# The first layer's scale vector by dot products on VectorE, its shift still by matrix products on TensorE

## The chip, the core and the metric

The kernel runs on one NeuronCore of a Trainium2 chip. The metric is the device time of one execution in microseconds (us), lower is better. The engines are named as the profile names them: PE is TensorE (PEld its weight loads), DVE is VectorE, ACT is ScalarE, POOL is GpSimd, and SP is the engine whose queue issues nearly all DMAs.

## What is computed

Two layers of a trunk over 128 context and 512 latent tokens of width 1024. Every layer is modulated by vectors that are made from two conditioning vectors (one for context, one for latent tokens) and a weight matrix `w_mod`. The change touches only how the first two of these vectors are made for the first layer.

```python
mod_ctx = (silu(c_ctx) @ w_mod[l] + b_mod[l])        # 6 * 1024 values
mod_lat = (silu(c)     @ w_mod[l] + b_mod[l])
sh1, sc1, gt1, sh2, sc2, gt2 = split(mod, 6)
h = rmsnorm(x, g_pre_mix) * (1 + sc1) + sh1
... = split_in(h @ w_in)                              # all branches of the layer start here
```

`sh1` is called the shift and `sc1` the scale below. Nothing of layer 0 can start on PE before `h` exists, and `h` needs both.

## The kernel before

Activations are kept transposed: 8 tiles `x[k]` of 128 channels by 640 tokens. A weight block is 128 output columns by 1024 inputs (512 KB). It is loaded into a ring of three buffers called `raw`, and `wblock` splits it into a high part `wh` (a cast on ACT) and a low part `wl` (a subtraction on DVE or POOL). `h[k]` is split likewise by `split`, a cast on ACT and a subtraction on DVE, and each product is three matmuls: high by high, high by low, low by high.

The order of work is not written by hand. A recorder collects all operations, and `schedule` places them by a list scheduler with modelled costs and due times. Nearly every instruction is issued through line 529, so rows are told apart by tile names, not by lines. Every engine then runs its own list in order.

The prologue (lines 923 to 975) is what the change touches:

- The 8 tiles of x are loaded, squared on ACT and summed, and `stat` makes the rms factor `rsb` of every token with small matmuls on PE and a power on POOL.
- `conv_blocks(0)` loads and splits the first four weight blocks of `win`. They are used by `first_k`, which adds one tile `h[k]` into seven accumulators: for 256 tokens four products (`pp` tiles, 12 matmuls of 256 columns), for the other 384 tokens three (`ps` tiles, 9 matmuls of 384 columns). `proj_half` makes the eighth accumulator, 24 more matmuls of 384 columns.
- For every k, the loop of line 951 makes the scale (j = 1) and then the shift (j = 0) of 128 channels. `half_tiles` loads the 512 KB block of `wmod0` as two tiles `u` of 256 KB, and 8 float32 matmuls of 2 columns each (`ps<-cc,u`; the trace has two records for each, so 16) add into two columns of one PSUM tile `gp`. A DVE instruction adds the bias (`mod<-ps,par`). `der` is (1 + scale) * gain. ACT then makes x * der + shift (two instructions, 512 and 128 tokens), and `split` gives `h[k]`.
- `cond()` loads `crow`, the two conditioning vectors spread over all partitions, into `cb` and applies Silu. It stands behind the loop, since before the change only the later vectors need it.

Those later vectors are made by `modvec`: one 512 KB block in a `raw` buffer, and two dot products on DVE (`tensor_tensor_reduce`; `CUSTOM_DVE_ANT_0` in the trace, `ISA` in the lists of order), one with each conditioning vector. The first dot writes its unused product to a `junk` tile, the second over the block itself, after which the buffer is free.

The first work behind the prologue is the key projection of head 0: products of 320 columns with the fifth weight block of `win`.

Of the kernel before, what the change touches and what calls it, by code (L numbers as in the profile page):

```python
# [11 lines left out]
F32 = mybir.dt.float32  # L12
F32R = mybir.dt.float32r
AF = mybir.ActivationFunctionType
ALU = mybir.AluOpType
AX = mybir.AxisListType

P = 128
D = 1024
KD = D // P  # L20
# [36 lines left out]
NSUM = 2  # L57
# [475 lines left out]
def trunk_kernel(ctx: ExitStack, tc: tile.TileContext, xT, crow, ccol, wmod, wmod0, win, wv, wa, wc, wattn, wo, wff1, wff2,  # L533
# [4 lines left out]
    nc = Recorder(tc.nc)  # L538

    def pool(name, bufs=1, psum=False):  # L540
        kw = dict(space=bass.MemoryType.PSUM) if psum else {}
        return Pool(ctx.enter_context(tc.tile_pool(name=name, bufs=bufs, **kw)), bufs, psum)
# [3 lines left out]
    wp = pool("wp")  # L546
    up = pool("up")
    sm = pool("sm")
# [6 lines left out]
    def nm(s):  # L555
        uid[0] += 1
        return f"{s}_{uid[0]}"

    def U(dt=F32, w=T):
        return up.tile([P, UW], dt, tag="U", name=nm("u"), bufs=NU)[:, :w]  # L560

    def PP():
        return psP.tile([P, 2, 512], F32, tag="P", name=nm("pp"))

    def PS():
        return psS.tile([P, 512], F32, tag="S", name=nm("ps"))
# [218 lines left out]
    def hl():  # L785
        return U(F32R), U(F32R)
# [102 lines left out]
    cb = cst.tile([P, 2, D], F32, name="cb")  # L889

    def cond():
        for g in range(2):
            nc.sync.dma_start(cb[:, g], crow[:, g, :])
            nc.scalar.activation(cb[:, g], cb[:, g], AF.Silu)

    def modvec(l, st, j):

        p, mod, der = st
        part = sm.tile([P, KD, 2], F32, tag="part", name=nm("part"), bufs=2)
        for m in range(KD):  # L900
            r = raw_load(wmod[l, j * KD + m])
            for g in range(2):
                junk = r if g else wp.tile([P, KD * P], F32, tag="sum", name=nm("junk"), bufs=NSUM)
                nc.vector.tensor_tensor_reduce(out=junk, in0=r, in1=cb[:, g], op0=ALU.mult, op1=ALU.add, scale=1.0,
                                               scalar=0.0, accum_out=part[:, m, g:g + 1])
            yield
        sl = mod[:, j * KD:(j + 1) * KD, :]
        o = OFF["b_mod"][0] + j * KD
        nc.vector.tensor_add(sl, part, p[:, o:o + KD, None].to_broadcast([P, KD, 2]))
        which = {1: (0, "g_pre_mix"), 2: (1, "g_post_mix"), 4: (2, "g_pre_mlp"), 5: (3, "g_post_mlp")}.get(j)  # L910
        if which is not None:
            i, gn = which
            g = pr(p, gn)[:, :, None].to_broadcast([P, KD, 2])
            if j in (1, 4):
                nc.vector.scalar_tensor_tensor(der[:, i], sl, 1.0, g, op0=ALU.add, op1=ALU.mult)
            else:
                nc.vector.tensor_mul(der[:, i], sl, g)
# [7 lines left out]
    p, mod, der = st[0]  # L925
# [5 lines left out]
    cc = sm.tile([P, KD, 2], F32, tag="cc", name=nm("cc"), bufs=1)  # L931
    nc.sync.dma_start(cc, ccol.rearrange("p (a b) -> p a b", b=2))
    nc.scalar.activation(cc, cc, AF.Silu)
    rsb = U()
    for a, b in PART:
        ((rs, _, _),) = stat(sq, a, b, inv[D], True, cuts=((0, b - a),))
# [1 line left out]
    wbs = conv_blocks(0)  # L938
    h = [hl() for _ in range(KD)]
    gp = PS()  # L940
    ts = [PP() for _ in range(2)]
    lead = [[ts[i // 2][:, i % 2, :TP] for i in range(4)], [PS()[:, :T - TP] for _ in range(3)]]
    DH = D // 2

    def half_tiles(src):
        r = [U(w=DH) for _ in range(2)]
        for i in range(2):
            nc.sync.dma_start(r[i], src[:, i * DH:(i + 1) * DH])
        return r

    for k in range(KD):
        nc.either.tensor_mul(x[k], x[k], rsb)
        for j in (1, 0):
            i0 = j * KD + k
            r = half_tiles(wmod0[i0])
            sl = mod[:, i0, :]
            o = OFF["b_mod"][0] + i0
            nc.begin()
            for i in range(KD):
                c = (i % 4) * P  # L960
                nc.tensor.matmul(gp[:, 2 * i0:2 * i0 + 2], r[i // 4][:, c:c + P], cc[:, i, :], start=(i == 0),
                                 stop=(i == KD - 1))
            nc.done()
            nc.vector.tensor_scalar(sl, gp[:, 2 * i0:2 * i0 + 2], p[:, o:o + 1], None, op0=ALU.add)
        o = OFF["g_pre_mix"][0] + k
        nc.vector.tensor_scalar(der[:, 0, k, :], mod[:, KD + k, :], 1.0, p[:, o:o + 1], op0=ALU.add, op1=ALU.mult)
        t = U()
        for s, e, g in ((0, TC, 0), (TC, T, 1)):
            nc.scalar.activation(t[:, s:e], x[k][:, s:e], AF.Identity, bias=mod[:, k, g:g + 1], scale=der[:, 0, k, g:g + 1])
        split(t, *h[k])  # L970
        for hf in range(2):
            first_k(lead[hf], wbs, h, hf, k)
    nc.sync.dma_start(rp, rope)
    cond()
    lead[1].append(proj_half(wbs[3], h, 1, parts=PART))
    xsrc = xT

    for l in range(DEPTH):
        p, mod, der = st[l]
# [33 lines left out]
        for hf in range(2):  # L1013
            for j in range(2):
                pg, pa = lead[hf][2 * j:2 * j + 2]
                a = PART[hf][0]
                for s, e, _ in PSEG[hf]:
                    o = gt[j][:, pos(s):pos(s) + e - s]
# [25 lines left out]
        for i in range(2):  # L1044
            nc.vector.tensor_tensor_reduce(out=U(w=QK), in0=lv[:, 2 * i], in1=lv[:, 2 * i + 1], op0=ALU.mult,
                                           op1=ALU.add, scale=1.0, scalar=0.0, accum_out=ls[:, i:i + 1])
# [215 lines left out]
        for it in range(NH + 1):  # L1262
# [18 lines left out]
            if pend is not None:  # L1281
                hd = it - 1
                pa, pc, ps0 = pend
                o = values(pa, pc, v[0][hd % 2], v[1][hd % 2])
# [95 lines left out]
        o = []  # L1380
        for hd in range(NH):
            r = U()
# [27 lines left out]
        m = []  # L1410
# [170 lines left out]
def _blocks(w):  # L1581

    K, M = w.shape
    return w.reshape(K // P, P, M // P, P).transpose(2, 1, 0, 3).reshape(M // P, P, K)
# [35 lines left out]
def _layout(inp):  # L1620
    a = {k: np.asarray(v) for k, v in inp.items()}
    L = DEPTH
    out = {}
    xall = np.concatenate([a["x_prompt"][0], a["x_sample"][0]], 0)
    out["xT"] = xall.T.reshape(KD, P, T)
    out["crow"] = np.broadcast_to(np.stack([a["c_ctx"], a["c"][0]])[None], (P, 2, D))
    out["ccol"] = np.stack([a["c_ctx"], a["c"][0]], 1).reshape(KD, P, 2).transpose(1, 0, 2).reshape(P, 2 * KD)
    w0 = a["w_mod"][0][:, :2 * D]
    out["wmod0"] = _blocks(w0)
    out["wmod"] = a["w_mod"].transpose(0, 2, 1).reshape(L, 6 * KD, P, D)  # L1630
    win, wv = [], []
    for l in range(L):
        w = a["w_in"][l]
        qp = (np.arange(2 * NH)[:, None] * QK + _DPERM[None]).reshape(-1)
        cols = np.concatenate([np.arange(0, 1536), 1536 + qp, 2560 + qp, np.arange(4608, 8704)])
        win.append(_blocks(w[:, cols]))
        v = w[:, 3584:4608].reshape(2, 4, P, 4, 2 * P)
        wv.append(v.transpose(3, 0, 2, 1, 4).reshape(8, P, D))
    out["win"] = np.stack(win)
    out["wv"] = np.stack(wv)  # L1640
    out["wa"] = np.stack([_pairs(a["sc_w_out"][l]) for l in range(L)])
    out["wc"] = np.stack([_pairs(a["cf_w_out"][l]) for l in range(L)])
    out["wattn"] = np.stack([_blocks(a["attn_w_out"][l]) for l in range(L)])
    out["wo"] = np.stack([_blocks(a["w_o"][l]) for l in range(L)])
    f0, f1 = FD * P, (NF - FE) * P
    out["wff1"] = np.stack([np.concatenate([_blocks(w[:, :f0]), _quads(w[:, f0:], KD)]) for w in a["w_ff1"]])
    ff2 = []
    for w in a["w_ff2"]:
        ff2.append(np.concatenate([_quads(w[:f1], KD), _blocks(w[f1:])]))
    out["wff2"] = np.stack(ff2)  # L1650

    def col(v):
        return v.reshape(-1, P).T

    pars = []
    for l in range(L):
        d = {
            "g_pre_mix": col(a["g_pre_mix"][l]), "g_post_mix": col(a["g_post_mix"][l]),
            "g_pre_mlp": col(a["g_pre_mlp"][l]), "g_post_mlp": col(a["g_post_mlp"][l]), "b_mod": col(a["b_mod"][l]),
            "sc_w": a["sc_conv_w"][l].reshape(SC_K, SCT, P).transpose(2, 1, 0).reshape(P, -1),  # L1660
            "cf_w": a["cf_conv_w"][l].reshape(CF_K, CFT, P).transpose(2, 1, 0).reshape(P, -1),
            "cf_b": col(a["cf_conv_b"][l]), "ln_g": col(a["cf_ln_g"][l]), "ln_b": col(a["cf_ln_b"][l]),
            "cf_b_out": col(a["cf_b_out"][l]), "subln": col(a["subln_g"][l]),
            "lam": np.broadcast_to(np.concatenate([a["lam_q1"][l], a["lam_k1"][l], a["lam_q2"][l], a["lam_k2"][l]])[None],
                                   (P, 4 * QK)),
        }
        pars.append(np.concatenate([d[n] for n, _ in PARAMS], 1))
    out["par"] = np.stack(pars)
    out["ck"] = a["cache_k"][0].transpose(0, 2, 3, 4, 1)[:, :, :, _DPERM].reshape(L, NH, P, P)
    out["cv"] = a["cache_v"][0].reshape(L, P, D)  # L1670
    out["rope"] = _rope_tables()
    return {k: np.ascontiguousarray(v) for k, v in out.items()}
# [28 lines left out]
```

## Time and profile before

| | us |
|---|---|
| median of 3 runs | 2597.32 (2591.19 to 2600.37) |
| the profiled execution | 2599.19 |
| span of its trace | 2597.4 |

PE is busy for 2488.8 us of the span. The profile's page gives busy time for each engine and for 40 equal slices of the span, the TensorE clock that was granted in each, and the chain of waits that ended last. The prologue is the first two slices of 65 us.

### The profile page before, as it was taken

The page shows a single profiled execution, that of the slowest core. Times are in us where ns is not written, and L with a number is a line of the kernel's source. Part 1 is how long each engine was busy: PE and PEld are TensorE (multiplying, and loading weights), DVE is VectorE, ACT ScalarE, POOL GpSimd, SP SyncE. Part 2 cuts the span into 40 slices and gives each one's busy share as a digit, 9 for nine tenths or more (in the row PEclk, how much of TensorE's full clock was granted, in tenths as well). Part 3 has the DMA queues.
Part 4 walks back from the last instruction along what each step waited for, and adds up shares of the span by engine and source line. Part 5 has one row for each costly group of instructions (what it writes and reads, how often), then busy time and mean ns, then how long its engine had stood idle before and what let it go on. Part 6 is the DMA issues. An engine that isn't in the chain of part 4 may idle for free.

```text
span 2597.4 us, 42157 instructions
## 1 busy us (share of the span) xinstructions
PE 2488.8 (96%) x16596; PEld 2412.5 (93%) x16596; DVE 1911.8 (74%) x3104; ACT 1250.4 (48%) x2323; POOL 290.7 (11%) x227
## 2 busy tenths in 40 slices
PE   7999999999999999999999999999999999999998
PEld 7988889999999899998988888999999999999998
DVE  3289786977785698878566887969566748677874
ACT  3365564223223566765445655532232247667653
POOL 1022110001020100012011211000011100001121
PEclk8899999999999999999989999999999999999999
DMA  7122222235554344577523222213454532447671
GB/s 269 48 93 65 66 68 71 87 127 194 176 178 138 99 166 175 191 176 187 171 87 97 76 62 77 73 56 115 154 174 137 175 110 96 140 156 210 176 216 56
DMA packets 132875, 336.76 MB, mean 130 GB/s; under 512 B 16244, under 2 KB 39108, under 8 KB 132676
## 3 DMA queue, kind: packets, MB, share of 16 engines
q1 hardware_dynamic: 122308, 315.19, 36.5%
q0 software_dynamic: 10368, 18.88, 4.3%
q8 instruction: 130, 2.13, 0.3%
q14 instruction: 69, 0.57, 0.1%
HBM read 284.15 MB, written 41.46 MB: 125 GB/s over the span
## 4 chain that ended last, share of the span: by engine, by line
PE 77%; DVE 11%; DMA 5%; ACT 4%; issue 2%; SPq 1%; POOL 0%; DVEq 0%; ACTq 0%; POOLq 0%
PE ps L529 41%; PE pp L529 35%; DVE u L529 8%; ACT u L529 3%; DMA raw<-in_wff_dram 2%; DMA u<-fd 2%; DVE w L529 1%; ACT w L529 1%; DVE mx L529 1%; DMA u<-u 1%; DVE sum L529 1%; SPq L529 1%; DMA u<-on 0%; DMA u<-rqd 0%; POOL st L529 0%
## 5 line engine op out<-in xcount | busy, mean ns | idle before, releaser
L529 PE MATMUL pp<-u,w 128*128 128x320 f32 (+1 forms) x6912 | 1069.6, 312 | 26.3 <-DVE u L529 12.9
L529 PE MATMUL ps<-u,w 128*128 128x320 f32 (+2 forms) x6672 | 1066.2, 315 | 12.1 <-DVE u L529 6.9
L529 PEld LDWEIGHTS pp<-u,w 128*128 128x128 f32 x6912 | 1030.1, 191 | 35.4 <-ACT u L529 13.6
L529 PEld LDWEIGHTS ps<-u,w 128*128 128x128 f32 x6672 | 1010.0, 191 | 25.0 <-DVE u L529 9.2
L529 ACT CAST w<-raw 128x1024 fp32r<-128x1024 f32 (+1 forms) x364 | 313.7, 863 | 290.2 <-PE ps L529 154.6
L529 DVE TENSOR_TENSOR w<-raw,w 128x1024 fp32r<-128x1024 f32 (+1 forms) x271 | 302.6, 1118 | 170.1 <-ACT w L529 166.7
L529 DVE TENSOR_TENSOR u<-u,u 128x640 fp32r<-128x640 f32 (+8 forms) x443 | 324.3, 744 | 72.8 <-ACT u L529 68.4
L529 ACT CAST u<-u 128x640 fp32r<-128x640 f32 (+2 forms) x280 | 195.5, 703 | 156.2 <-DVE u L529 79.7
L529 DVE SCALAR_TENSOR_TENSOR u<-u,par,u 128x640 f32<-128x640 f32 (+13 forms) x272 | 225.8, 863 | 1.7
L529 ACT ACTIVATE u<-u 128x320 f32<-128x320 f32 (+3 forms) x232 | 138.6, 612 | 117.8 <-DVE u L529 109.3
L529 DVE TENSOR_TENSOR w<-sum,w 128x512 fp32r<-128x512 f32 x208 | 143.4, 697 | 43.2 <-ACT w L529 42.2
L529 ACT CAST w<-sum 128x512 fp32r<-128x512 f32 x208 | 127.2, 621 | 87.2 <-PE pp L529 36.5
L529 ACT ACTIVATE u<-pp 128x640 f32<-128x640 f32 (+4 forms) x96 | 52.1, 552 | 234.1 <-PE pp L529 223.3
L529 POOL TENSOR_TENSOR u<-u,u 128x640 f32<-128x640 f32 (+4 forms) x60 | 104.6, 1747 | 503.2 <-DVE u L529 302.1
L529 DVE TENSOR_TENSOR u<-u,ps 128x320 f32<-128x320 f32 (+4 forms) x230 | 106.7, 481 | 52.8 <-PE ps L529 52.2
L529 DVE TENSOR_TENSOR u<-ps,u 128x512 fp32r<-128x512 f32 (+6 forms) x206 | 98.3, 505 | 59.8 <-PE ps L529 33.9
L529 DVE CUSTOM_DVE_ANT_0 junk<-raw,cb 128x1024 f32<-128x1024 f32 x80 | 102.5, 1283 | 46.7 <-DMA raw<-in_wmod_dram 46.5
L529 POOL DMA_DIRECT2D w<-in_wff_dram x72 | 62.9, 873 | 612.9 <-DVE sum L529 361.6
L529 PE MATMUL ps<-w,u 128*128 128x256 f32 x960 | 127.7, 291 | 2.8 <-ACT vo L529 2.8
L529 ACT ACTIVATE u<-pp,mx 128x640 f32<-128x640 f32 x128 | 101.0, 793 | 58.4 <-DVE mx L529 57.4
L529 PEld LDWEIGHTS ps<-w,u 128*128 128x128 f32 x960 | 120.9, 197 | 6.9 <-ACT vo L529 4.0
L529 POOL TENSOR_TENSOR w<-raw,w 128x1024 fp32r<-128x1024 f32 x21 | 52.9, 2521 | 565.6 <-ACT w L529 459.9
(90 smaller groups left out, 1874.5 us busy)
## 6 DMA issues: line engine op xcount, KB each, us to landing
raw<-in_wff_dram SPq DMA_DIRECT2D x128, 512.0 KB, 3.9
raw<-in_win_dram SPq DMA_DIRECT2D x120, 512.0 KB, 3.3
raw<-in_wmod_dram SPq DMA_DIRECT2D x80, 512.0 KB, 3.4
fd<-u SPq DMA_DIRECT2D x64, 320.0 KB, 2.4
u<-fd SPq DMA_DIRECT2D x64, 320.0 KB, 5.6
w<-in_wff_dram POOLq DMA_DIRECT2D x72, 256.0 KB, 5.8
u<-in_wmod_dram SPq DMA_DIRECT2D x32, 256.0 KB, 6.1
raw<-in_wv_dram SPq DMA_DIRECT2D x16, 512.0 KB, 3.3
```

The source lines that it names most:

```text
L529: getattr(eng, m)(*[r(v) for v in a], **{x: r(v) for x, v in k.items()})
```

## The change

The scale blocks of `wmod0` are stored transposed, loaded into the `raw` ring as 512 KB tiles, and multiplied with the two rows of `cb` by two dot products on DVE (a new helper `dots`, taken out of `modvec`). The shift is made as before. `cond()` moves ahead of the loop.

```diff
+    def dots(r, out):
+        for g in range(2):
+            junk = r if g else wp.tile([P, KD * P], F32, tag="sum", name=nm("junk"), bufs=NSUM)
+            nc.vector.tensor_tensor_reduce(out=junk, in0=r, in1=cb[:, g], op0=ALU.mult, op1=ALU.add, scale=1.0,
+                                           scalar=0.0, accum_out=out[:, g:g + 1])
...
     nc.scalar.activation(cc, cc, AF.Silu)
+    cond()
...
+    part = sm.tile([P, KD, 2], F32, tag="part", name=nm("part"), bufs=2)
...
         for j in (1, 0):
             i0 = j * KD + k
-            r = half_tiles(wmod0[i0])
             sl = mod[:, i0, :]
             o = OFF["b_mod"][0] + i0
-            nc.begin()
-            for i in range(KD):
...
+            if j == 0:
+                r = half_tiles(wmod0[i0])
+                nc.begin()
+                for i in range(KD):
...
+            else:
+                r = raw_load(wmod0[i0])
+                dots(r, part[:, k])
+                nc.vector.tensor_scalar(sl, part[:, k], p[:, o:o + 1], None, op0=ALU.add)
...
     nc.sync.dma_start(rp, rope)
-    cond()
```

The scheduler places the whole prologue anew. From the key projection of head 0 on, PE's list is the same but for ten rows that change places, and the other lists but for a few.

PE, before: the middle of the prologue, at x[3]. `ps_236` is `gp`, `u_153` to `u_175` are half blocks of `wmod0`, `w_..` the split weights, `pp_300`, `ps_331` and `ps_338` accumulators of `first_k`.

```order
L529 MATMUL ps_236<-cc_125,u_153 128x2 x4
L529 MATMUL ps_236<-cc_125,u_155 128x2 x4
L529 MATMUL ps_331<-u_421,w_234 128x384
L529 MATMUL ps_331<-u_423,w_234 128x384
L529 MATMUL ps_331<-u_421,w_246 128x384
L529 MATMUL ps_338<-u_421,w_249 128x384
L529 MATMUL ps_338<-u_423,w_249 128x384
L529 MATMUL ps_338<-u_421,w_254 128x384
L529 MATMUL ps_236<-cc_125,u_157 128x2 x4
L529 MATMUL ps_236<-cc_125,u_175 128x2 x4
L529 MATMUL pp_300<-u_480,w_198 128x256
```

PE, now: the end of the shift's matmuls for x[1], those for x[2], and the first for x[3] (`ps_234` is `gp`), with the semaphores that each waits for.

```order
L529 MATMUL ps_234<-cc_128,u_132 128x2 x3
L529 MATMUL ps_234<-cc_128,u_134 128x2 [waits DMAHW2_49]
L529 MATMUL ps_234<-cc_128,u_134 128x2 x3
L529 MATMUL ps_234<-cc_128,u_136 128x2 [waits DMAHW3_49,DVE_49]
L529 MATMUL ps_234<-cc_128,u_136 128x2 x3
L529 MATMUL ps_234<-cc_128,u_138 128x2 [waits DMAHW4_49]
L529 MATMUL ps_234<-cc_128,u_138 128x2 x3
L529 MATMUL ps_234<-cc_128,u_140 128x2 [waits DMAHW5_49,DVE_49]
```

Seven of the eight shift groups (x[0] to x[6]) now stand in one row ahead of the first product, and the eighth stands in the middle of the products of x[6]; before, sixteen groups stood between the products. As before, the first matmul of a group waits for DVE, from the third group on.

DVE, before: the middle of the prologue.

```order
L529 TENSOR_SCALAR mod_272<-ps_236,par_127 128x2
L529 TENSOR_TENSOR u_296<-u_291,u_294 128x640
L529 TENSOR_SCALAR mod_272<-ps_236,par_127 128x2
L529 TENSOR_SCALAR der_274<-mod_272,par_127 128x2
L529 TENSOR_SCALAR mod_272<-ps_236,par_127 128x2
L529 TENSOR_TENSOR u_353<-u_336,u_351 128x640
```

DVE, now: from the split of the fourth weight block (`w_298`) to the scale of x[0] (`der_330`). `raw_200` and `raw_224` are the scale blocks of x[0] and x[1].

```order
L529 TENSOR_TENSOR w_298<-raw_177,w_294 128x1024 [waits DMAHW7_49,Activation_49]
L529 ISA junk_308,part_309<-raw_200,cb 128x1024 [waits DMAHW1_49]
L529 ISA part_309 128x1
L529 TENSOR_SCALAR mod_260<-ps_234,par_130 128x2 [waits PE_49]
L529 ISA raw_200,part_309<-raw_200,cb 128x1024 [waits DVE_49]
L529 ISA part_309 128x1
L529 ISA junk_323,part_309<-raw_224,cb 128x1024 [waits DMAHW4_49]
L529 ISA part_309 128x1
L529 TENSOR_SCALAR mod_260<-part_309,par_130 128x2 [waits DVE_49]
L529 TENSOR_SCALAR mod_260<-ps_234,par_130 128x2 [waits PE_49]
L529 ISA raw_224,part_309<-raw_224,cb 128x1024 [waits DVE_49]
```

Between the splits of h now stand sixteen dots, and between the dots the bias instructions of the shift, which wait for PE.

## Rows read from the trace of the kernel before

**Rows 1.** The page, part 2: TensorE's granted clock in 40 slices, tenths.

```profile
PEclk8899999999999999999989999999999999999999
```

**Rows 2.** Stretches (start:end, length), busy us of PE, PEld, DVE, ACT, POOL; clock, DMA share, GB/s.

```profile
20.00:40.00 20.00, 16.40 (x83) 15.94 (x84) 10.95 (x14) 5.70 (x8) 6.31 (x5) 1.00 1.04 394
...
60.00:80.00 20.00, 20.00 (x108) 20.00 (x108) 3.30 (x10) 5.01 (x9) 0.00 (x0) 0.64 0.00 0
...
86.20:91.60 5.40, 5.40 (x22) 5.40 (x23) 1.39 (x4) 1.93 (x3) 0.00 (x0) 0.51 0.00 0
91.60:95.20 3.60, 3.60 (x32) 3.60 (x31) 0.00 (x0) 0.00 (x0) 0.00 (x0) 1.00 0.00 0
102.00:107.40 5.40, 5.40 (x36) 5.40 (x35) 3.68 (x7) 4.59 (x9) 0.00 (x0) 1.00 0.16 44
132.60:136.00 3.40, 1.97 (x13) 1.54 (x11) 3.15 (x2) 1.74 (x5) 2.04 (x1) 1.00 0.34 86
```

**Rows 3.** Groups by line and shape, 0 to 125 us: the 2-column matmuls.

```profile
L529 PE MATMUL ps<-cc,u 128*128 128x2 f32 x256 | 43.4, 302 | 1.0 <-DVE mod L529 1.0
```

**Rows 4.** Timeline, PE (start us, us, instructions, idle before and its releaser).

```profile
19.10 6.83 PE L529 MATMUL ps<-cc,u 128*128 128x2 f32 x32
26.95 3.58 PE L529 MATMUL ps<-cc,u 128*128 128x2 f32 x16 [1.02 <-DVE mod L529]
...
86.22 2.91 PE L529 MATMUL pp<-u,w 128*128 128x256 f32 x12
...
91.67 1.58 PE L529 MATMUL pp<-u,w 128*128 128x256 f32 x12
93.08 0.69 PE L529 MATMUL ps<-u,w 128*128 128x384 f32 x3
93.61 3.63 PE L529 MATMUL ps<-cc,u 128*128 128x2 f32 x32
97.10 3.15 PE L529 MATMUL ps<-u,w 128*128 128x384 f32 x12
...
102.67 7.50 PE L529 MATMUL ps<-u,w 128*128 128x384 f32 x45
...
107.36 0.90 PE L529 MATMUL ps<-u,w 128*128 128x320 f32 x5
```

**Rows 5.** Timeline, ACT, DVE and POOL, 7 to 34 us.

```profile
7.61 4.01 ACT L529 ACTIVATE u<-u 128x640 f32<-128x640 f32 x5 [0.25 <-DMA u<-in_xT_dram]
...
19.72 1.05 ACT L529 CAST w<-raw 128x1024 fp32r<-128x1024 f32 x1
...
19.91 6.18 POOL L529 TENSOR_TENSOR u<-u,u 128x640 f32<-128x640 f32 x3 [2.30 <-ACT u L529]
20.06 2.16 DVE L529 TENSOR_TENSOR u<-u,u 128x640 f32<-128x640 f32 x1
...
26.69 0.21 DVE L529 TENSOR_SCALAR mod<-ps,par 128x2 f32<-128x2 f32 x1
...
30.57 0.22 DVE L529 TENSOR_SCALAR mod<-ps,par 128x2 f32<-128x2 f32 x1 [1.21 <-PE ps L529]
...
30.82 1.20 ACT L529 ACTIVATE u<-u,mod,der 128x512 f32<-128x512 f32 x2 [10.05 <-DVE mod L529]
32.05 0.72 ACT L529 CAST u<-u 128x640 fp32r<-128x640 f32 x1
...
32.81 0.82 DVE L529 TENSOR_TENSOR u<-u,u 128x640 fp32r<-128x640 f32 x1 [2.02 <-ACT u L529]
```

**Rows 6.** Instructions on `junk` (ns min/median/max), and DVE's timeline from 500 us.

```profile
L529 DVE CUSTOM_DVE_ANT_0 junk<-raw,cb x80: 1210/1224/2596, 503.1 to 2058.2; 128x1024 f32<-128x1024 f32 x80
...
504.61 1.22 DVE L529 CUSTOM_DVE_ANT_0 raw<-raw,cb 128x1024 f32<-128x1024 f32 x1
505.75 0.08 DVE L529 DVE_READ_ACCUMULATOR2_ANT part<- 128x1 f32 x1
```

**Rows 7.** Loads into `raw` in the first 60 us: issue to landing.

```profile
DMA to landing us min/median/max: 3.3/5.9/7.4
```

More of the change, by code (lines that the diff above doesn't have):

```diff
@@ L901, in modvec @@
             r = raw_load(wmod[l, j * KD + m])
[L902 to L905, printed above, removed]
+            dots(r, part[:, m])
             yield
@@ L954, in trunk_kernel @@
             i0 = j * KD + k
-            r = half_tiles(wmod0[i0])
             sl = mod[:, i0, :]
             o = OFF["b_mod"][0] + i0
-            nc.begin()
-            for i in range(KD):
[L960 to L964, printed above, removed]
+            if j == 0:
+                r = half_tiles(wmod0[i0])
+                nc.begin()
+                for i in range(KD):
+                    c = (i % 4) * P
+                    nc.tensor.matmul(gp[:, 2 * i0:2 * i0 + 2], r[i // 4][:, c:c + P], cc[:, i, :], start=(i == 0),
+                                     stop=(i == KD - 1))
+                nc.done()
+                nc.vector.tensor_scalar(sl, gp[:, 2 * i0:2 * i0 + 2], p[:, o:o + 1], None, op0=ALU.add)
+            else:
+                r = raw_load(wmod0[i0])
+                dots(r, part[:, k])
+                nc.vector.tensor_scalar(sl, part[:, k], p[:, o:o + 1], None, op0=ALU.add)
         o = OFF["g_pre_mix"][0] + k
@@ L1628, in _layout @@
     w0 = a["w_mod"][0][:, :2 * D]
-    out["wmod0"] = _blocks(w0)
+    out["wmod0"] = np.concatenate([_blocks(w0[:, :D]), w0[:, D:].T.reshape(KD, P, D)])
     out["wmod"] = a["w_mod"].transpose(0, 2, 1).reshape(L, 6 * KD, P, D)
```

## The prediction

> **What bounds the kernel now.** I read the granted clock over the span first [rows 1]: it is lower in the first two slices (and one later), so the prologue is where PE loses time. The stretches [rows 2] show two parts in it. Until 40 us the DMA engines are full (394 GB/s). From 60 to 80 us PE is busy throughout at a mean clock of 0.64, while nothing is loaded and DVE has 3.3 us of work in 20: PE is the bound. The timeline of PE [rows 4] shows with what: between the products stand the 2-column matmuls, 256 records and 43.4 us of PE [rows 3]. They cost twice. [...] And the stretches that hold them are mostly at the low level: with the products alone PE came to 1.00 after 5.4 us, from 86.2 to 91.6 and had it from there to 95.2 [rows 2], and kept it where only products follow (102.0 to 107.4). One tile h[k] in all its 21 products costs 5.45 us at the low level (86.22 to 91.67) and 2.98 at the high one: 12 of 256 columns from 91.67 to 93.08, 1.41, and 9 of 384 at 0.174, since 27 of them stand between 102.67 and 107.36 [rows 4].
>
> The prologue ends for PE where the first product of head 0 starts, at 107.4 us [rows 4]. Behind this point PE's list is the same, so what this start gains is the gain, unless something later doesn't move with it.
>
> **What the change removes.** Eight of sixteen groups, 128 of the 256 records, half of 43.4 us = 21.7 us at the mixture of clocks that they had. And it moves seven of the remaining eight ahead of the first product, where PE had little to do.
>
> **What it adds.** Sixteen dots on DVE. One takes 1.22 us, the next instruction starts 1.14 after it (504.61, 505.75) [rows 6]; I take 1.2 with its wait for the one before. So 19.2 us, on an engine with 16 us free in 20 [rows 2]. The largest dot took 2.6 us; POOL at work beside it would explain that, as it does for the multiplication that took 2.16 at 20.06 while POOL had three [rows 5].
>
> Now the new prologue, forward from the loads, in us of the span.
>
> *Start of the shift groups.* Two weight blocks (1.05 MB) now stand among the loads of x: at 394 GB/s x[7] lands 2.7 later, and its square ends up to 2.7 behind the 11.62 of now. But ACT and DVE split these two blocks (a cast takes 1.05) while they wait for x, which stood behind the squares before [rows 5]. The rms factors therefore come between 0 and 2.7 later than now (19.91, where POOL starts to use them); I take 1.2, in the middle. The first group starts at 19.1 + 1.2 = 20.3.
>
> *The shift groups.* The third group of before ran at 26.95, right after the bias instruction at 26.69; the bias of the second group (ended at 25.93) waited at 30.57 for the third to end [rows 4, 5]. So writes and reads of this PSUM tile exclude each other in turn: a group waits for the last bias, a bias for the last group. The two lists keep that. Seven groups at 3.41 = 23.9; from the third on a bias lies between two, 5 x 0.25 = 1.25. The bias of x[3] stands behind the fourth weight block's split and the first dot: 34.7 (bias of x[2]) + 0.7 for small ones + cast 1.05 + subtraction 1.2 + dot 1.2 = 38.9, where the group before it ended at 38.2: 0.7 more. Sum: 20.3 + 23.9 + 1.25 + 0.7 = 46.2 for the first product. DVE and ACT come to the same point: dot 2 of x[0], dot 1 of x[1], the bias of x[4] (waits for its group, 42.6), dot 2, der: 44.2; two ACT instructions 1.2 and a cast 0.72 [rows 5]: 46.1. Before, the first product came at 32.8.
>
> *From there to the end of the prologue.* PE has 8 x 2.98 = 23.8, 24 matmuls of 384 for the eighth accumulator at 0.174 = 4.2, and the eighth group 1.75. Until the clock rises, the first 5.4 us are at half speed: 2.7 more. DVE has from 44.2 twelve dots (14.4), eight splits of h at 0.82 (6.6) and some 17 small ones at 0.2 (3.5): 24.5 us, until 68.7, with up to 1.3 more while POOL splits a weight block. That is close to PE, so PE waits now and then. Followed tile by tile, h[2] is whole at about 57, while PE is through with h[1] at 46.2 + 5.5 + 3.0 = 54.7: a gap of 2.2; h[4] and h[5] come 0.5 late each. Sum of the waits 3.2. h[7] needs the shift of the eighth group, which PE runs inside the products of x[6]: bias, ACT 1.92 and split 0.82 fit beside the rest of these products (2.6) and three others (0.5). The end: 46.2 + 23.8 + 4.2 + 1.75 + 2.7 + 3.2 = 81.9.
>
> The gain is 107.4 - 81.9 = 25.5 us. The profiled execution took 2599.2; less 25.5 gives 2573.7. It lies 1.9 above the median of the three runs, so against the median I say 2572.
>
> *What is hidden, and its cover.* The loads: the scale block of x[0] ends the first 11.0 MB of loads, which take 28 us at 394 GB/s; with some 4 us for the start and the landing it is there at 32, its first dot is due at 37.7: cover 5 us. From x[2] on a block needs a buffer of the ring whose second dot is done, and lands 3.3 to 7.4 later [rows 7]; three buffers are used in turn, so a buffer has the time of two other blocks, some 7 us, for it. At 7.4 a dot would wait 0.4 us, a few times: 2 us. `cond()`: 1 MB of load ahead of the shift blocks, whose groups are paced by PE (cover: the shift block of x[5] ends 8.7 MB, so it lands at about 26 by the same count, and its group starts at 39), and 2 us of ACT, before the factors are due. The fifth to eighth weight blocks come behind the scale blocks, the fifth at about 62, split on POOL by 69; it is due at 81.9, cover 13 us.
>
> **Rivals.**
> *The clock doesn't come up.* In the new order PE waits between tiles. Were the products at the low level throughout: 46.2 + 8 x 5.45 + 24 x 0.31 + 3.4 = 100.6 (0.31 is 2.75 / 9, from the same tile at 86.22), a gain of 7; half of them, about 17. Against it: from 132.6 to 136.0 PE was busy for only 1.97 of 3.4 us, at a clock of 1.00 [rows 2]. [...]
> *PE isn't paced by the groups.* Were they at the high level (1.75) or without the turn-taking, DVE sets the pace: blocks split at 32.4, first dots there, 5.3 earlier than above, last split 63.4, then h[7] 3.0 and 21 matmuls 3.7: about 71, a gain of 36. Against it: the rows at 19.10 and 26.95.
> *Slower.* The ring could work as if it had one buffer, if a block were asked for only when the one before is done: load 5.9 + two dots 2.4 + small 0.7 + split 0.8 = 9.8 for each of eight, from 37.7: 116, and ACT, h[7] and the rest 9.4 behind it: 125.5, 18 us slower, 2615. It turns to a loss from (107.4 - 9.4 - 37.7) / 8 = 7.5 us for a block. Against it: three buffers.
> *The gain is given back later*, where a wait doesn't move with PE. Nothing in the stretch behind 107 stands still in time; 2597.
>
> **How the numbers follow.** Forecast with its own range of 20 to 31 us of gain, 0.70; clock partly low (7 to 20) 0.13, wholly low 0.03; DVE's pace (31 to 38) 0.09; given back 0.02; slower 0.03. Own range of the forecast: 2566 to 2577. The range takes in most of the partly low clock and of DVE's pace: 2561 to 2584. A measurement of this kernel tells 0.3% (7.8 us) from no change: faster 0.92, same 0.05, slower 0.03.
>
> **What would show it.** In the trace after: seven groups of 3.4 us in a row from about 20 with biases between; the first 256-column product near 46; clock 1.00 from about 52 with short gaps of PE, released by DVE or ACT; sixteen dots from 38 to 68 at 1.2 each; the first 320-column product near 82. The prediction is wrong if the clock between 50 and 80 has a mean under 0.8, if dots wait for their loads, if a dot takes 2 us in the mean, or if the time from that product to the end isn't what it was (2597.4 - 107.4 = 2490).

## The result, and the profile after

The changed kernel takes 2570.25 us (median of 4 runs, 2564.94 to 2573.44) against 2598.85 for the kernel before, measured beside it (median of 4, 2591.19 to 2600.73): the ratio is 0.989, with a 95% interval of 0.9871 to 0.991. The forecast was 2572. The profiled execution took 2568.82 us, its span is 2567.1, and the first 320-column product, which ends the prologue, starts at 81.57 us; before it started at 107.36 [rows 4]. From there to the end it is 2567.1 - 81.57 = 2485.5 us, before 2490.0.

The granted clock over the span (page, part 2) has lost its lower start [rows 1]:

```profile
PEclk9999999999999899999989999999999998999999
```

Two stretches (columns as in [rows 2]):

```profile
60.00:80.00 20.00, 19.52 (x134) 18.99 (x134) 12.62 (x26) 12.30 (x21) 2.91 (x1) 1.00 0.28 91
53.40:81.50 28.10, 27.62 (x189) 27.09 (x189) 20.47 (x39) 17.85 (x29) 2.91 (x1) 1.00 0.37 123
```

From 60 to 80 us PE is nearly as busy as before (19.52 of 20 us), at a clock of 1.00 where it had 0.64 [rows 2], and DVE works 12.6 us where it worked 3.3. How the groups of PE changed, by shape, from 17 us to the end of the prologue:

```profile
L529 PE MATMUL ps<-cc,u 128*128 128x2 f32 x128 | 26.5, 339 | 1.7 <-DVE mod L529 1.7
L529 PE MATMUL ps<-u,w 128*128 128x384 f32 x96 | 19.2, 351 | 0.0
L529 PE MATMUL pp<-u,w 128*128 128x256 f32 x96 | 15.0, 304 | 0.9 <-DVE u L529 0.9
```

and the same view of the kernel before:

```profile
L529 PE MATMUL ps<-u,w 128*128 128x384 f32 x96 | 24.7, 407 | 0.0
L529 PE MATMUL pp<-u,w 128*128 128x256 f32 x96 | 22.1, 401 | 2.9 <-ACT u L529 2.3 <-DVE u L529 0.6
```

The 2-column groups take 26.5 us where they took 43.4 [rows 3], 16.9 less. The 192 products are the same in number and take 34.2 us where they took 46.8, 12.6 less: that is the clock, 1.00 where it was 0.64 from 60 to 80 us. Together 29.5; 25.8 arrives (107.36 - 81.57), since the groups start 2.1 later and PE waits elsewhere.

PE's timeline:

```profile
21.21 6.83 PE L529 MATMUL ps<-cc,u 128*128 128x2 f32 x32
28.34 3.57 PE L529 MATMUL ps<-cc,u 128*128 128x2 f32 x16 [0.31 <-DVE mod L529]
...
43.99 3.57 PE L529 MATMUL ps<-cc,u 128*128 128x2 f32 x16 [0.31 <-DVE mod L529]
47.43 0.56 PE L529 MATMUL pp<-u,w 128*128 128x256 f32 x1
48.42 2.71 PE L529 MATMUL pp<-u,w 128*128 128x256 f32 x11 [0.43 <-DVE u L529]
50.93 2.85 PE L529 MATMUL ps<-u,w 128*128 128x384 f32 x9
53.62 1.57 PE L529 MATMUL pp<-u,w 128*128 128x256 f32 x12
55.02 1.73 PE L529 MATMUL ps<-u,w 128*128 128x384 f32 x9
56.59 1.59 PE L529 MATMUL pp<-u,w 128*128 128x256 f32 x12
...
69.57 0.50 PE L529 MATMUL pp<-u,w 128*128 128x256 f32 x2 [0.47 <-DVE u L529]
69.91 1.84 PE L529 MATMUL ps<-cc,u 128*128 128x2 f32 x16
...
81.57 0.60 PE L529 MATMUL ps<-u,w 128*128 128x320 f32 x3
```

Seven groups in a row, 3.41 to 3.58 us each, DVE's bias between them from the third on. I call this the low level's length, since in the kernel before a group took it in a stretch with a granted clock of 0.50 (columns as in [rows 2]), while two took 3.49 together, the high level's length, at 1.00 (93.61 to 97.10 [rows 4]):

```profile
61.03 3.41 PE L529 MATMUL ps<-cc,u 128*128 128x2 f32 x16
61.03:64.30 3.27, 3.27 (x18) 3.27 (x17) 1.14 (x3) 1.74 (x3) 0.00 (x0) 0.50 0.01 3
```

For the seven groups the clock is given as 1.00 (21.2 to 46.5 us), and for the first tile's products too (47.4 to 53.6), though they go at the low level's pace (2.71 for 11). From 53.6 on the products go at the high one (1.57 for 12, 1.73 for 9). And DVE, first at the start of the dots, then at the one place behind the first tile where it holds up PE (POOL beside it):

```profile
38.69 1.22 DVE L529 CUSTOM_DVE_ANT_0 junk<-raw,cb 128x1024 f32<-128x1024 f32 x1
39.84 0.08 DVE L529 DVE_READ_ACCUMULATOR2_ANT part<- 128x1 f32 x1
...
63.59 2.91 POOL L529 TENSOR_TENSOR w<-raw,w 128x1024 fp32r<-128x1024 f32 x1 [37.35 <-ACT w L529]
64.16 2.37 DVE L529 TENSOR_SCALAR der<-mod,par 128x2 f32<-128x2 f32 x1
66.44 1.21 DVE L529 CUSTOM_DVE_ANT_0 raw<-raw,cb 128x1024 f32<-128x1024 f32 x1
66.70 1.20 ACT L529 ACTIVATE u<-u,mod,der 128x512 f32<-128x512 f32 x2 [3.19 <-DVE der L529]
```

A two-column instruction, 0.22 us elsewhere, takes 2.37 and ends at 66.53, as POOL's subtraction does (66.50). ACT waits for it, and behind ACT the split of h[6] and PE (the 0.47 at 69.57).

### The profile page after: what moved, and what is told of

The parts are those of the page before. It is cut to its first block, busy times and chain, and to the rows that moved or that the text cites. A ratio compares the mean times of both kernels' runs of the same rounds, so it can differ in the third digit from the quotient of the medians.

```text
span 2567.1 us, 41907 instructions
## 1 busy us (share of the span) xinstructions
PE 2459.7 (96%) x16468; PEld 2383.4 (93%) x16468; DVE 1926.1 (75%) x3136; ACT 1249.1 (49%) x2323; POOL 292.1 (11%) x227
## 3 DMA queue, kind: packets, MB, share of 16 engines
q1 hardware_dynamic: 121156, 315.19, 37.1%
## 5 line engine op out<-in xcount | busy, mean ns | idle before, releaser
L529 PE MATMUL pp<-u,w 128*128 128x320 f32 (+1 forms) x6912 | 1059.8, 310 | 25.8 <-ACT u L529 12.2
L529 DVE CUSTOM_DVE_ANT_0 junk<-raw,cb 128x1024 f32<-128x1024 f32 x88 | 111.9, 1273 | 48.5 <-DMA raw<-in_wmod_dram 48.2
```

The source lines that it names most:

```text
L529: getattr(eng, m)(*[r(v) for v in a], **{x: r(v) for x, v in k.items()})
```

## The experiments

What a whole run tells is coarse: in the profiles below the stretch behind the first 320-column product takes between 2475.7 and 2493.7 us (the span less that start), and for one and the same kernel it differs by up to 10. The start itself is sharper, so the table gives both; times are medians, ratios against the kernel before, measured beside each.

| kernel | first product | first 320-col. product | rest of span | time | ratio (95%) |
|---|---|---|---|---|---|
| before (a profile of it, another) | 32.8, 32.85 | 107.36, 112.19 | 2490.0, 2480.0 | 2598.85, 2594.98 | 1 |
| changed (three profiles) | 47.43, 48.12, 47.83 | 81.57, 83.78, 83.62 | 2485.5, 2475.7, 2483.4 | 2570.25, 2567.3, 2567.86 | 0.989 (0.9871 to 0.991) |
| one extra group a tile | 51.25 | 98.23 | 2491.9 | 2585.68 | 0.9965 (0.9945 to 0.9986) |
| two extra groups a tile | 53.06 | 135.31 | 2480.5 | 2617.13 | 1.0066 (1.0042 to 1.009) |
| sixteen groups ahead, no dots | 76.21 | 107.03 | 2486.8 | 2596.0 | 0.9991 (0.9977 to 1.0006) |
| one bias (two profiles) | 48.87, 48.66 | 79.51, 79.73 | 2482.8, 2486.9 | 2574.25, 2571.78 | 0.9921 (0.9896 to 0.9946) |
| six groups, one bias (two) | 41.66, 41.94 | 75.59, 75.72 | 2493.7, 2489.3 | 2572.2, 2568.51 | 0.9909 (0.988 to 0.9938) |
| all by dots | 40.64 | 89.61 | 2486.8 | 2575.66 | 0.9921 (0.9894 to 0.9949) |
| before, `cond()` early | 32.23 | 106.81 | 2480.1 | 2597.22 | 1.0006 (0.9989 to 1.0022) |

My theory was that the groups cost twice: their own time on PE, and the clock of the products around them. The first three experiments are on that; the next three on what else sets the prologue's end.

### One extra group for every tile

The changed kernel with eight more groups, one for each tile; a group reads the tile that ACT has made, and the scheduler placed each one ahead of its tile's products. Their results are not used.

```diff
+        nc.begin()
+        for i in range(KD):
+            c = (i % 5) * P
+            nc.tensor.matmul(gp[:, 2 * (KD + k):2 * (KD + k) + 2], t[:, c:c + P], cc[:, i, :], ...)
+        nc.done()
```

> The changed kernel, with eight groups of sixteen 2-column matmul records put back on PE between the products, one for each tile; they read the tile that ACT has just made and their result is not used. Loads, dots and biases stay. My theory (the groups between the products cost PE their own time and also pull its clock down): the first 320-column product comes 14 us (8 x 1.75, clock at 1.00 throughout) to 30 us later, with the mean clock from 48 to 100 us below 0.9; whole run 2588 (2583 to 2600). Rival A (own time alone): 14 us later at a clock of 1.00, 2584. Rival B (DVE's dots set the pace and PE has room): under 8 us later, under 2578.

The prologue ended at 98.23, 16.7 us later than in the first profile of the changed kernel. PE's timeline and one stretch:

```profile
61.22 1.84 PE L529 MATMUL ps<-cc,u 128*128 128x2 f32 x16
62.92 1.67 PE L529 MATMUL pp<-u,w 128*128 128x256 f32 x12
...
84.07 1.84 PE L529 MATMUL ps<-cc,u 128*128 128x2 f32 x16
...
87.46 1.95 PE L529 MATMUL ps<-cc,u 128*128 128x2 f32 x16 [0.39 <-ACT u L529]
89.27 2.23 PE L529 MATMUL pp<-u,w 128*128 128x256 f32 x12
```

```profile
58.00:87.00 29.00, 29.00 (x225) 28.75 (x224) 11.56 (x24) 7.43 (x12) 2.90 (x1) 1.00 0.24 76
58.00:98.00 40.00, 39.61 (x286) 39.29 (x286) 17.19 (x33) 14.54 (x23) 2.90 (x1) 0.96 0.21 69
```

With one group in a tile the clock stays at 1.00 (58 to 87 us). Seven of the extra groups cost their own 1.70 us (61.22 to 62.92), and that of x[0] stands ahead of the first product, where a group takes 3.41: 7 x 1.70 + 3.41 = 15.3 of the 16.7 us. At one place two groups come close together, the shift group of x[7] (84.07; its bias follows at 85.95) and the extra one of x[7] (87.46); behind them twelve products take 2.23 us in place of 1.67, and the mean clock up to 98 us is 0.96. So this comes nearest to rival A, the own time alone (14 us later at a clock of 1.00, 2584 us expected). The mean clock below 0.9 that my theory expected did not come: of its second half hardly anything is to be seen at this dose.

### Two extra groups for every tile

The same with a second group behind the first, so that each tile has two, as in the kernel before.

> Two extra groups of 2-column matmuls (16 matmuls, 32 records) for every tile h[k], placed after its products, as two groups stood in the kernel before; their results are not used. One extra group a tile left the granted clock at 1.00 and cost its own 1.84 us each. Theory A (two groups in a row between the products pull the clock down, as in the kernel before, where a tile with two groups took 9.3 us): tiles of about 9 us, first 320-column product at 125 to 137 us, run 25 to 35 us above the kernel with one extra group. Rival (only their own time at the high level, 32 groups of records at 1.75 each pair of eight): 16 x 1.75 = 28 us more than the 81.6 of the changed kernel, and 2 to 5 for a later start, so 111 to 116 us, run 2598 to 2604.

The prologue ended at 135.31, within what the theory expected and far from the rival's 111 to 116.

```profile
61.43 3.50 PE L529 MATMUL ps<-cc,u 128*128 128x2 f32 x16 [1.17 <-DVE mod L529]
64.79 2.91 PE L529 MATMUL pp<-u,w 128*128 128x256 f32 x12
...
69.48 4.73 PE L529 MATMUL ps<-cc,u 128*128 128x2 f32 x32
74.06 2.91 PE L529 MATMUL pp<-u,w 128*128 128x256 f32 x12
```

```profile
53.00:135.30 82.30, 81.13 (x433) 81.04 (x434) 19.97 (x42) 16.27 (x26) 0.00 (x0) 0.69 0.12 40
```

The 256-column products of every tile run at the low level (2.91 for 12), and the clock's mean is 0.69, with PE busy for 81.13 of 82.30 us: its one wait is the 1.17 at 61.43, and the falls behind that come without any. By the end of the prologue the first extra group of a tile cost 16.7 / 8 = 2.1 us, the second 37.1 / 8 = 4.6 (135.31 - 98.23). So the second half of the theory holds, but in these kernels only above one group a tile: with two groups of 16 to the 21 products of a tile the clock came down (0.69), with one it stayed up (1.00 from 58 to 87 us).

### All sixteen groups ahead of the first product

The kernel before with its groups moved out of the products, and one bias instruction behind them; no dots.

```diff
+    for i0 in range(2 * KD):
+        r = half_tiles(wmod0[i0])
+        nc.begin()
+        for i in range(KD):
+            nc.tensor.matmul(gp[:, 2 * i0:2 * i0 + 2], r[i // 4][:, c:c + P], cc[:, i, :], ...)
+        nc.done()
+    nc.vector.tensor_add(mod[:, 0:2 * KD, :], gp[:, 0:4 * KD]..., p[:, o:o + 2 * KD, None]...)
```

> All sixteen groups stay on PE, but ahead of the first product, with one bias instruction behind them; no dots on DVE. Theory A (the gain is PE time that is removed, and the groups ahead of the products cost the low level's 3.41 us each): groups from about 19 to 74, first product near 76, products at the high level but for the first 5.4 us, first 320-column product at 105 to 110: no gain. Rival C (the gain comes from moving the groups out of the products, so that the clock stays up): 85 to 95 and a gain of 12 to 22 us.

It ended at 107.03: no gain, as the first theory said. By shape, from 17 us to that end, and PE's timeline:

```profile
L529 PE MATMUL ps<-cc,u 128*128 128x2 f32 x256 | 54.6, 351 | 0.0
L529 PE MATMUL ps<-u,w 128*128 128x384 f32 x96 | 18.7, 344 | 0.0
L529 PE MATMUL pp<-u,w 128*128 128x256 f32 x96 | 14.4, 301 | 3.4 <-ACT u L529 3.1 <-DVE u L529 0.3
```

```profile
21.91 51.20 PE L529 MATMUL ps<-cc,u 128*128 128x2 f32 x240
76.21 0.58 PE L529 MATMUL pp<-u,w 128*128 128x256 f32 x1 [3.10 <-ACT u L529]
77.06 2.71 PE L529 MATMUL pp<-u,w 128*128 128x256 f32 x11 [0.28 <-DVE u L529]
...
81.72 1.58 PE L529 MATMUL pp<-u,w 128*128 128x256 f32 x12
```

The products got the clock (33.1 us against 46.8, 13.7 less; 1.00 from 82 to 107 us), but the groups all took 3.41, 54.6 us against 43.4, 11.2 more; the clock is given as 1.00 for them as well (22 to 73 us). Moving groups is worth next to nothing; the gain of the change is the eight groups that PE no longer has, 107.03 - 81.57 = 25.5 at this place. The kernel of the next section has one bias as well and differs from this one by those eight groups, their dots and the early `cond()`: its end comes 27.5 us earlier (107.03 to 79.51), and eight groups of 3.41 are 27.3.

### One bias instruction

The changed kernel with all eight shift groups ahead and one bias behind them, so that no group waits for a bias.

```diff
+    nc.vector.tensor_add(mod[:, 0:KD, :], gp[:, 0:2 * KD]..., p[:, o:o + KD, None]...)
-                nc.vector.tensor_scalar(sl, gp[:, 2 * i0:2 * i0 + 2], p[:, o:o + 1], None, op0=ALU.add)
```

> The changed kernel, with one bias instruction for all eight shift groups in place of eight. So groups and biases no longer take turns. My theory (after the first product PE's own work sets the end): eight groups of 3.41 us without gaps from about 19.2 us, then bias 0.2, ACT 1.9; first 256-column product at 48.6; then 8 x 2.98 + 24 x 0.174 + 2.7 for the clock + 0.5: first 320-column product at about 80 (81.5 in the changed kernel), whole run 1 to 2 us faster than the changed kernel, 2567 to 2571. Rival (DVE's dots set the pace): DVE is free of PE from 22 us on, dots start 5 us earlier, first 320-column product at 76 or earlier, 2565 or less.

```profile
22.16 23.89 PE L529 MATMUL ps<-cc,u 128*128 128x2 f32 x112
48.87 0.58 PE L529 MATMUL pp<-u,w 128*128 128x256 f32 x1 [2.82 <-ACT u L529]
49.73 2.72 PE L529 MATMUL pp<-u,w 128*128 128x256 f32 x11 [0.28 <-DVE u L529]
...
54.35 1.58 PE L529 MATMUL pp<-u,w 128*128 128x256 f32 x12
```

The turn-taking is gone (seven groups of 16 in 23.89 us without a gap). The first product is later by 1.4, since h[0] now needs the bias behind the eighth group, but from 49.73 on PE runs to the end of the prologue without a wait, and it comes at 79.51 (in a second profile at 79.73): 30.6 us behind the first product, where PE's own work is 23.8 + 4.2 + 2.7 = 30.7 by the prediction's terms. PE's work sets this end, not DVE. The whole run did not show it: 2574.25 and 2571.78 us, where 2567 to 2571 was expected.

### Six groups and one bias

The shift of x[6] and x[7] by dots too: six groups on PE, twenty dots on DVE.

```diff
+    NG = 6
...
-        for j in (1, 0):
+        for j in ((1,) if k < NG else (1, 0)):
...
+            r = raw_load(wmod0[i0] if j else wmod[0, i0])
+            dots(r, pt[:, k])
```

> One bias instruction for the shift groups, and only six groups on PE; the shift of x[6] and x[7] goes to DVE as four more dots (20 in all). Theory A (PE's work sets the end of the prologue, DVE has a few us to spare): two groups of 3.41 us less on PE ahead of the first product, so first product near 42, and first 320-column product at 76 to 80 us (79.6 with eight groups and one bias); DVE, which ended its last split at 67.9, gets 4.8 more. Rival B (DVE is already at the edge): the four dots delay h[6] and h[7] and the product comes at 80 to 84. The run, 2562 to 2574, differs from the changed kernel by no more than a measurement can tell.

```profile
41.66 0.58 PE L529 MATMUL pp<-u,w 128*128 128x256 f32 x1 [2.39 <-ACT u L529]
42.95 2.72 PE L529 MATMUL pp<-u,w 128*128 128x256 f32 x11 [0.71 <-DVE u L529]
...
68.77 1.58 PE L529 MATMUL pp<-u,w 128*128 128x256 f32 x11 [0.47 <-DVE u L529]
```

The prologue ended at 75.59, slightly under the 76 expected and 6.0 before the changed kernel's: theory A. Whether the whole run has this gain was the question of a second measurement, with the changed kernel, the one-bias kernel and the kernel before beside it:

> The kernel with six groups and one bias once more, beside the changed kernel, to see whether the 6 us that its prologue is shorter (first 320-column product at 75.6 us against 81.6) reach the end. If they do (the rest of the run doesn't depend on when the prologue ends): the rest takes 2480 to 2490 us and the run is 4 to 8 us under the changed kernel's. If they are given back behind the prologue: the rest takes 2490 or more again (2493.7 in its first profile) and the two runs are equal within 2 us.

> The changed kernel a third time, for the comparison with the six-group kernel: 2565 to 2575 us; the rest behind the first 320-column product 2475 to 2490 us (2485.5 and 2475.7 in the two profiles so far).

> Eight groups and one bias instruction once more: prologue end at 79 to 80 us; if what the prologue gains reaches the end, 1 to 3 us under the changed kernel, else equal to it or above, as its first median was.

> The kernel before, for a second profile of it: first 320-column product at 106 to 108 us, the rest 2480 to 2492 us (2490.0 in the first profile). If the rest is shorter by the same few us in all kernels of this call, it goes with the chip and not with the kernel.

The six-group kernel took 2568.51 (2564.97 to 2574.86, ratio 0.9894, 0.9869 to 0.9919), the changed kernel 2567.86 (2564.82 to 2575.52; 0.9893, 0.987 to 0.9916), the one-bias kernel 2571.78 (0.9911, 0.9887 to 0.9934). The prologues are as short as in the first profiles (75.72, 83.62, 79.73), and the rest again is longer behind the short ones (2489.3 and 2486.9 against 2483.4). By the numbers set down the times are on the side of "given back" (equal within 2 us), while the rest of 2489.3 still lies in the range set for the other side; two profiles of the six-group kernel and a spread of 10 us in one kernel's rest can't tell it from chance. The kernel before ended its prologue at 112.19, not at the 106 to 108 expected, and the rests of the four kernels, from 2480.0 to 2489.3, do not move together. Six groups beat the kernel before; against the changed kernel the case stays open.

### Everything by dots

No group on PE: the shift by dots as well, 32 dots on DVE.

```diff
-            if j == 0:
+            if j == 0 and False:
...
+                r = raw_load(wmod0[i0] if j else wmod[0, i0])
+                dots(r, pt[:, k])
```

> The changed kernel, with the shift made by dots on DVE too: no 2-column matmuls of weights on PE, 32 dots in place of 16, 16 blocks of 512 KB through the ring of three. My theory (in the changed kernel PE and DVE are near balance, so DVE becomes the bound): DVE has 32 x 1.2 + 6.6 + some 11 of small and x work from about 21 us, so h[7] at 80, first 320-column product at 85 to 90, whole run 2574 to 2579, still some 20 us faster than before. PE idles about half of the time between the tiles, and the clock may be low there without cost. Rival (PE's groups are the bound by far and DVE has room): first 320-column product at 70, 2559. Rival (the ring of three sets the pace, one block per 5 us): 21 + 80 + 9 = 110, no faster than before.

```profile
44.89 3.86 PE L529 MATMUL ps<-u,w 128*128 128x384 f32 x12
54.34 0.58 PE L529 MATMUL pp<-u,w 128*128 128x256 f32 x1 [5.59 <-ACT u L529]
55.70 2.72 PE L529 MATMUL pp<-u,w 128*128 128x256 f32 x11 [0.78 <-DVE u L529]
```

```profile
40.60:89.60 49.00, 36.61 (x192) 33.90 (x193) 44.41 (x79) 17.70 (x28) 12.73 (x6) 0.90 0.46 152
```

The first product comes earlier than in the changed kernel, at 40.64, and the end, 89.61, later: DVE is busy for 44.41 of 49.0 us, and PE waits for ACT and DVE behind it. Not all of this is the number of dots. The scheduler gave POOL subtractions in this stretch (12.73 us, 2.91 in the changed kernel), and five dots beside them took 2.54 to 2.58 us each (40.86, 45.90, 48.40, 56.71 and 79.02) in place of 1.22, 6.7 more in all. So sixteen dots are on the good side of the balance and 32, as they were scheduled here, beyond it.

### Only the order of the loads

The kernel before with `cond()` moved ahead of the loop and nothing else.

> The kernel before, with only the move of cond() ahead of the loop, so that the two conditioning rows are loaded and activated early. Nothing else of the change. My theory (the gain is PE's time and clock, not the order of loads): the same as before within 0.15%, the first 320-column product at 107 to 109. Rival (the new order of loads and ACT work gives a part of the gain): 5 us or more faster.

The prologue ended at 106.81, just under the 107 to 109 expected, and the ratio is 1.0006: the move costs and brings nothing by itself.

### The changed kernel again

> The changed kernel once more, for a second profile and for times beside those of the others on the same chip: 2565 to 2575 us, first 320-column product at 80 to 83 us; what follows it to the end within 2480 to 2492 (2485.5 in the first profile).

It took 2567.3 (2561.26 to 2573.43). The prologue ended at 83.78 and the rest took 2475.7, both outside what was expected (80 to 83, and 2480 to 2492). Of the 2.2 us against the first profile 0.7 is there before the shift group of x[7] (70.62 against 69.91), 0.5 of it around a wait for h[2] (0.27 idle, at 57.31) that the first profile doesn't have. The other 1.5 come behind this group:

```profile
70.62 1.84 PE L529 MATMUL ps<-cc,u 128*128 128x2 f32 x16
...
73.54 3.73 PE L529 MATMUL ps<-u,w 128*128 128x384 f32 x12
77.11 1.58 PE L529 MATMUL pp<-u,w 128*128 128x256 f32 x12
```

Twelve products took 3.73 us, the low level (0.31 each; the clock is 0.74 from 70.6 to 77.1), where they took 2.26 in the first profile, with the same program and the same wait just ahead (0.47 and 0.48). In the third profile the twelve were slow there as well (3.40), and PE waited 0.44 for h[2]. The kernel before has such luck too: its two profiles end the prologue at 107.36 and 112.19, with a clock of 0.64 and 0.59 from 60 to 80 us, in which PE is busy throughout in both.

## Why the prediction was right, point by point

**Where the gain comes from.** It said 25.5 us in the prologue and none behind it. The first pair of profiles gives 25.8; the means of all profiles of the two kernels give (107.36 + 112.19) / 2 - (81.57 + 83.78 + 83.62) / 3 = 26.8. The rest of the span is 2485.0 and 2481.5 in the mean, nearer than two profiles of one kernel. The first measurement's 4.5 us in it (2490.0 to 2485.5) can be chance by the spread in the table, and the 28.6 us between the medians are in part this luck.

**That the groups cost twice** is right, and the runs say how: their own time (1.70 for a group at a clock of 1.00, at 61.22 with one extra group a tile; 3.41 at 0.50, at 61.03 in the kernel before) and, where two stand in a tile, the clock (4.6 for the second). What I had not seen is that moving groups ahead of the first product is no gain by itself: seven, eight and sixteen of them in a row all had the low level's length (3.41 to 3.58). The forecast of seven groups at 3.41 came from two at 19.10 [rows 4], which show the length but not how long it lasts; that it held for all seven is what the runs showed, not what those rows did. Why a group takes 3.41 there, while the clock is given as 1.00, no run shows.

**The shift groups.** Forecast: start 20.3, first product 46.2; measured 21.21 and 47.43. The start was 0.9 late (the middle of a bound of 0 to 2.7), the way from there 26.2 against 25.9. The turn-taking was read rightly, and its price was near: from the third group on a group starts 3.89 behind the one before (28.34 to 32.23), 0.48 above 3.41, where I had 0.25, and the bias of x[3] cost 0.1 in place of 0.7 (an idle time of 0.41 in place of 0.31); together 2.35 against 1.95. Taking it away moved the first product by nothing to the good, since the bias then waited for all eight groups, and, with the eighth group out of the products of x[6], brought 2 to 4 us at the end of the prologue (81.57 to 83.78 against 79.51 and 79.73).

**From the first product to the end.** The terms and what they measured: eight tiles of 2.98 (from 53.62 to 56.59, 2.97); the clock's rise, 2.7 forecast: 21 products fill 47.43 to 53.62, 6.19 us, of which 0.43 is a wait and 2.98 their time at the high level, so 2.8; the eighth group 1.75, half of the 3.49 from 93.61 to 97.10 [rows 4], measured 1.70 (69.91 to 71.61). The step that failed is "a gap of 2.2" at h[2], and with it the "sum of the waits 3.2": PE met h[2] without a wait at 56.59, since PE was there 1.9 later than I had it and DVE's split 0.5 earlier. In the other two profiles it did wait there, for 0.27 and 0.44. The waits were 0.43 and 0.47, with 0.29 of the weight loads (at 68.71), 1.2 in all. That the end still came at 81.57 instead of 81.9 is luck: a first product 1.2 late against waits that were too long by 2.0, which makes 81.1; these terms don't place the other 0.4.

**The dots.** 1.22 each with the next start 1.15 later (38.69 to 39.84), none waited for its block. The term that was mis-sized is "up to 1.3 more while POOL splits a weight block": it was 2.37 - 0.22 = 2.15, on the smallest kind of instruction, where I had thought of the dots. The trace shows the two side by side: POOL began 0.57 us before DVE's instruction (63.59 and 64.16), which ended 0.03 us after POOL's (66.53 and 66.50). What holds DVE there no row shows. The "some 4 us for the start and the landing" of the loads was my estimate; ACT took up the first tile of x at 3.82 us before and at 3.55 now.

**The rivals.** "The clock doesn't come up" was wrong for this order: 1.00 from 53.4 to 81.5 with waits of at most 0.47, and a fall behind the eighth group that cost 1.5 us in the second profile and 1.6 in the third (from the start of this group to the end of the prologue 11.7, 13.2 and 13.3 us). That PE's waits between the tiles would keep the clock low was not shown: products at the low level stand behind a wait of 5.59 us in the kernel with everything by dots (2.72 for 11 at 55.70), but also ahead of it (3.86 for 12 at 44.89); and in the kernel with two extra groups PE's only wait is the 1.17 us at 61.43, and the clock falls again and again long behind it (a mean of 0.69 from 53.0 to 135.3). "PE isn't paced by the groups" was wrong: with six groups in place of eight the first product came 7.2 us earlier than with eight and one bias (48.87 to 41.66; two groups are 6.8). "The ring works as one buffer" and "given back later" found no row in the changed kernel.

**What stays open.** Why the clock falls behind one single group in some executions and not in others; and whether the 6 us of the six-group kernel are lost behind the prologue or only in the spread. Every profile has the same 16115 matmul records in the rest, and PE is busy with them for 2386.4 to 2400.9 us and idle for 87.7 to 96.2, so both the pace of the same matmuls and the waits differ from one execution to the next.

## What to carry to other kernels

Price small matmuls by what they do to the clock of the work around them as well as by their own time, and by the dose: here, by the end of the prologue, one group in a tile cost 2.1 us and the second 4.6. Where PE was the bound and VectorE had room (20.00 and 3.30 of 20 us busy from 60 to 80 us, before the change), moving such work to VectorE paid here, but only to the balance: sixteen dots gave 26 us in the prologue, thirty-two, part of them slowed by POOL, gave 18. Judge an edit of one stage by where that stage ends in the trace; a whole run here could not tell 6 us.

## What the runs showed of the hardware

- 240 records of 2-column matmuls in a row, 51.20 us of PE without a gap, ran at the low level's pace to the end (0.213 us each; at the high level 16 take 1.70, 0.106 each), although the granted clock of the stretch is given as 1.00; the high level came only 5.5 us after the first 256-column product (76.21 to 81.72). The durations and the column of the clock disagree there, and no run shows why; I read the level from the durations.
- One instruction of DVE on 128 x 2 elements took 2.37 us beside a subtraction of POOL, ten times the 0.22 it takes elsewhere, at 64.16 in the first profile of the changed kernel and at 64.86 in the second; in the six-group kernel a dot took 2.59 beside POOL's 1.58 (61.67 and 61.60), elsewhere 1.22.
- The same program ended its prologue at 107.36 and at 112.19 us, with its first product at 32.8 and 32.85 and a granted clock of 0.64 and 0.59 from 60 to 80 us, where PE is busy throughout in both.
